# One of the weight sums of the seven-product pieces of the down projections and the last gate is made during the MLP halves, kept in DRAM, and read back into the weight piece

## The chip, the cores and the metric

One core of one Trainium2 chip runs the program. The metric is the device time of one execution in microseconds, lower is better. Of several executions the median is given.

## The reference

One encoder layer on 256 tokens of 2048 features, all in fp32. The parts that matter here:

```python
merged = jax.nn.sigmoid(ga) * (ya @ w_branch_a[i]) + jax.nn.sigmoid(gb) * (yb @ w_branch_b[i])
x = x + merged @ w_out[i]
hf = rms_norm(x, ffn_norm[i])
g = dwconv_centred(hf @ w_ffn_gate[i], conv_w[i], conv_b[i])
x = x + (jax.nn.gelu(g) * (hf @ w_ffn_up[i])) @ w_ffn_down[i]
gate_p = jax.nn.sigmoid(rms_norm(x, ple_norm[i]) @ w_ple_gate[i])
x = x + gate_p * (p[i] @ w_ple_proj[i])
```

Ahead of these stand the combined input projection and two kinds of windowed attention (ya, yb); a last rms norm follows. The feed-forward width is 5632.

## The kernel before, in words

**The stream of weights.** All weights lie in DRAM as 258 pieces of 128 x 2048 fp32 (1 MB, sixteen blocks of 128 x 128), in the order in which they are used. SyncE's DMA queue (SP) loads them into three buffers `raw` (L245); `produce` asks for piece p + 2 when it starts on piece p. A piece is cut into units, and each unit is split into two halves that TensorE can multiply in one pass: ScalarE (ACT) makes the high half (L265), VectorE (DVE) the low half, the rest (L266). The split units lie in two rings: "u" (tiles uh, ul) has 6 units, "v" (vh, vl) has 2. When TensorE has used a unit, `drop` frees its place and `pump` splits the next one. So ScalarE and VectorE run ahead of TensorE by what the rings hold, and no further.

**Stages in order.** A (projection and attention); B0 to B3 (the gates of the two branches), each followed by ba and bb (the branch projections); D0, D1 (the output projection and the residual); E0 (first half of the MLP's gate and up products) and F00, F01 (its down projection); E1, F10, F11 the same for the second half; pp0, pp1 (the projection of p); G0, G2, G3 (the last gate). In E a product uses one piece, 16 blocks, with a 512-wide and a 256-wide matmul for each; `mlp` then gathers it and, after every second one, does the convolution, gelu and the product of gate and up on VectorE and ScalarE.

**Pieces of seven products.** In B, D, F, G0 a piece holds two by two quarters of 128 x 512. `quad_stage` uses either eight products of quarters, kind "s", or seven, kind "S": the Winograd form of Strassen's method, where three of the seven use sums of weight quarters and four use sums of the moving side (tile S, made by `sums_of`). The sums of weights are made in place in `raw` by three subtractions on VectorE, once the plain quarters have been split (L258 to L260): first T1 and T3 (1024 wide), then T2 and the negative of T4 (512 wide each). The units that hold sums go through the ring "v". Each product is three matmuls (`thirds`, L366 to L368), so a seven-product piece is 21 matmuls of 512 columns. Of the 11 pieces of each F stage five are "S" (`DOWN`), of the 8 of G0 four (`ALT`).

**What sets the order.** The program text gives an order of emission; work can be put off to a place in a later stage with `at((stage, i, k), f)`. A scheduler then puts each engine's instructions in a fixed row by what each depends on and its own estimates, and may take one far ahead of its place in the text where its inputs and its buffer are free. On the chip each engine runs its row in order. Tiles with the same tag share a buffer and wait for each other. `act2` holds two rows of the MLP's activations, `S4` the moving sums of a pair of pieces.

Of the kernel before, what the change touches and what calls it, by code (L numbers as in the profile page):

```python
# [94 lines left out]
ALT = "SsSsSsSs"  # L95
DOWN = "SsSsSsSsSss"
FIRST_GATES = "ssssSsSs"
# [13 lines left out]
def _pieces():  # L111
# [29 lines left out]
    for half in range(2):  # L141
        names = {"g": "w_ffn_gate", "u": "w_ffn_up"}
        jobs = [(names[kind], f) for kind, f in _ffn(half)]
        joint = 0 if half else JOINT
        e = [(name, k, f) for k in range(KC) for name, f in jobs[:joint]]
        e += [(name, k, f) for name, f in jobs[joint:] for k in range(KC)]
        blocks("E%d" % half, e)
        for s in range(2):
            quads("F%d%d" % (half, s), ("w_ffn_down", 2 * s * WIDE), ("w_ffn_down", (2 * s + 1) * WIDE),
                  DOWN, half * FHALF)  # L150
# [14 lines left out]
def _unit_list():  # L165

    units, of = [], []
    for p, (kind, _) in enumerate(_PIECES):
        if p == 0:
            cuts = [("n", a * P, b * P) for a, b in ((0, 1), (1, 4), (4, 7), (7, 11), (11, PIECE))]  # L170
        elif kind == "S":
            cuts = [("n", 0, WIDE), ("n", 2 * WIDE, 4 * WIDE), ("T13", 0, 2 * WIDE), ("T24", 2 * WIDE, 4 * WIDE)]
        else:
            cuts = [("n", 0, 2 * WIDE), ("n", 2 * WIDE, 4 * WIDE)]
        of.append(list(range(len(units), len(units) + len(cuts))))
        units += [(p, *cut) for cut in cuts]
    return units, of
# [11 lines left out]
def _encoder(ctx: ExitStack, tc, xt, pt, xrow, cols, gainrow, table, onehot, mask, ident_in, wts, out):  # L189
# [13 lines left out]
    def bank(which, *shape):  # L203
# [7 lines left out]
        return ps.tile(list(shape) or [P, 2 * T], F32, name="bank", tag="b%d" % which, bufs=1)  # L211

    flat = big.tile([P, KC + KC * T], F32, name="x", tag="R1")
    x = flat[:, KC:].rearrange("p (k t) -> p k t", t=T)
# [27 lines left out]
    def load(r, a=0, b=PIECE):  # L242
        if a == 0:
            raws[r] = wpool.tile([P, PIECE * P], F32, name="raw", bufs=3)
        nc.sync.dma_start(raws[r][:, a * P:b * P], wts[r][:, a * P:b * P])  # L245
        state["raw"] = r + 1

    def produce():
# [7 lines left out]
        if kind == "T13":  # L256
            q = [raw[:, i * WIDE:(i + 1) * WIDE] for i in range(4)]
            nc.vector.tensor_tensor(raw[:, :2 * WIDE], raw[:, WIDE:3 * WIDE], raw[:, :2 * WIDE], op=ALU.subtract)  # L258
            nc.vector.tensor_tensor(q[2], q[2], q[0], op=ALU.subtract)
            nc.vector.tensor_tensor(q[3], q[3], q[2], op=ALU.subtract)  # L260
        src = raw[:, a:b]
# [3 lines left out]
        nc.scalar.activation(hi, src, AF.Copy)  # L265
        nc.vector.tensor_tensor(lo, src, hi.bitcast(F32), op=ALU.subtract)  # L266
        made[u] = (hi, lo)
        state["unit"] = u + 1
# [104 lines left out]
    def quad_stage(stage, moving, combos=None, tags=("M2", "M3", "M4", "P22")):  # L373
# [24 lines left out]
        for i, p in enumerate(pieces):  # L398
# [11 lines left out]
            else:  # L410
                s = combos(i)
                sums = [(s[:, 0, e], s[:, 1, e]) for e in range(4)]
                for g, (name, stationary, u, c, gone) in enumerate((
                        ("M1", part(a, 0), 0, 0, 0), ("M7", sums[2], 2, 1, None), ("M5", sums[0], 2, 0, 2),
                        ("M6", sums[1], 3, 0, None), ("M4", part(b, 1), 3, 1, 3),
                        ("M2", part(b, 0), 1, 1, None), ("M3", sums[3], 1, 0, 1))):
# [182 lines left out]
    def bias(h0, n):  # L599
# [8 lines left out]
    def view(a, offset, *dims):  # L608
        return bass.AP(tensor=a.tensor, offset=a.offset + offset, ap=[a.ap[0], *([step, n] for step, n in dims)])

# [357 lines left out]
    def mlp(kind, n, acc):  # L968
# [21 lines left out]
        else:  # L990
# [17 lines left out]
            pair = m // 2  # L1008
            if DOWN[pair] == "S":
                combos["act", pair] = sums_of(u, pair // 2)  # L1010
# [7 lines left out]
    def split_last():  # L1018
        for k in range(2):
# [3 lines left out]
            nc.vector.tensor_tensor(pl_[k], held["pr"][:, k], ph_[k].bitcast(F32), op=ALU.subtract)  # L1023

    for half in range(2):
        held["act"] = [big.tile([P, 16, 2 * T], FR, name="act", tag="R1"),
# [10 lines left out]
        turns["e"] = 0  # L1037
        for kind, n in jobs[joint:]:
            mlp(kind, n, product(stage, lambda k: hf[:, k, :], KC, "e"))
        if half:  # L1040
            at(("F10", 2, 0), load_last)
# [146 lines left out]
```

## Time and profile before

| | |
|---|---|
| median of 3 runs | 1457.01 us (1456.82 to 1458.02) |
| the profiled execution: its time | 1457.09 us |
| its span in the profile | 1455.3 us |
| mean granted clock of TensorE | 0.998 |
| HBM read, written | 279.49 MB, 2.14 MB |

The span is that from the first to the last instruction of the program; what lies around it is 1.8 us. In the profile a tile stands under its name in the program without its number, L266 is line 266 of the kernel shown. PE is TensorE's matmul, PEld its weight loads, SPq and ACTq the DMA issues of those queues. A group's row gives the count, then busy us and the mean ns of one, then the idle time of the engine in front of them with what ended it. A timeline row gives start, duration, engine, line, operation and tiles, and in brackets the idle time in front.

### The profile page before, as it was taken

How to read it: one execution, taken by the hardware profiler on the slowest of the kernel's cores; microseconds unless marked ns; L12 is line 12 of the kernel's file. 1: busy time of each engine (PE TensorE's matmuls, PEld its weight loads, DVE VectorE, ACT ScalarE, POOL GpSimd, SP SyncE). 2: the span in 40 equal slices, each digit the busy share in tenths (PEclk: the TensorE clock that was granted, in tenths of full speed). 3: DMA queues.
4: the chain of work that ended last, by engine and by line, in shares of the span. 5: the costliest groups of instructions: out<-in, count | busy, mean ns of one | idle time of the engine just before them, and what ended most of it. 6: DMA issues, size and time to landing. Idle time of an engine off the chain costs nothing.

```text
span 1455.3 us, 19303 instructions
## 1 busy us (share of the span) xinstructions
PE 1444.2 (99%) x7476; PEld 1234.3 (85%) x7476; DVE 1196.8 (82%) x1626; ACT 838.7 (58%) x1132; POOL 4.8 (0%) x9
## 2 busy tenths in 40 slices
PE   9999999999999999999999999999999999999997
PEld 8888888888888888888888888888888888888785
DVE  7677664679998989988787789987877778999994
ACT  7455544456555656666565565455655656565763
POOL 0000000000000000000000000000000000000000
PEclk9999999999999999999999999999999999999999
DMA  9653445535546456465555545465555554546462
GB/s 336 250 205 145 160 162 178 170 141 203 197 186 236 184 209 231 174 233 201 177 194 184 198 147 225 175 253 187 198 178 199 176 201 173 190 193 235 170 234 85
DMA packets 46455, 282.87 MB, mean 194 GB/s; under 512 B 4948, under 2 KB 9940, under 8 KB 14108
## 3 DMA queue, kind: packets, MB, share of 16 engines
q1 hardware_dynamic: 45644, 280.46, 52.8%
q8 instruction: 58, 0.95, 0.3%
q10 hardware_dynamic: 720, 1.19, 0.2%
q14 instruction: 33, 0.27, 0.1%
HBM read 279.49 MB, written 2.14 MB: 194 GB/s over the span
## 4 chain that ended last, share of the span: by engine, by line
PE 97%; DVE 1%; ACT 1%; issue 0%; DMA 0%; POOL 0%; POOLq 0%; DVEq 0%; SPq 0%; ACTq 0%
PE bank L309 29%; PE bank L316 15%; PE bank L366 14%; PE bank L367 14%; PE bank L368 14%; PE bank L355 2%; PE bank L357 2%; PE bank L293 2%; PE bank L356 2%; PE bank L294 1%; PE bank L861 1%; PE bank L678 0%; PE bank L626 0%; PE bank L625 0%; PE bank L624 0%
## 5 line engine op out<-in xcount | busy, mean ns | idle before, releaser
L265 ACT ACTIVATE uh<-raw 128x1024 fp32r<-128x1024 f32 (+2 forms) x519 | 523.1, 1015 | 394.0 <-PE bank L309 163.8
L266 DVE TENSOR_TENSOR ul<-raw,uh 128x1024 fp32r<-128x1024 f32 (+2 forms) x519 | 594.9, 1166 | 162.6 <-issue 81.0
L309 PE MATMUL bank<-hf,uh 128*128 128x512 f32 x1408 | 336.3, 391 | 0.0
L309 PEld LDWEIGHTS bank<-hf,uh 128*128 128x128 f32 x1408 | 258.9, 188 | 50.1
L316 PEld LDWEIGHTS bank<-hf,ul 128*128 128x128 f32 x1408 | 180.4, 191 | 6.7
L316 PE MATMUL bank<-hf,ul 128*128 128x256 f32 x1408 | 182.8, 283 | 0.0
L265 ACT ACTIVATE vh<-raw 128x1024 fp32r<-128x1024 f32 x92 | 97.0, 1056 | 42.4 <-DVE raw L258 22.9
L266 DVE TENSOR_TENSOR vl<-raw,vh 128x1024 fp32r<-128x1024 f32 x92 | 111.8, 1218 | 0.3
L309 PE MATMUL bank<-hs,uh 128*128 128x512 f32 x432 | 103.6, 392 | 0.0
L447 ACT ACTIVATE t<-bank 128x256 f32<-128x256 f32 x122 | 46.5, 383 | 97.4 <-PE bank L316 86.5
L309 PEld LDWEIGHTS bank<-hs,uh 128*128 128x128 f32 x432 | 79.5, 188 | 15.6
L366 PE MATMUL bank<-uh,act 128*128 128x512 f32 x232 | 90.4, 390 | 0.0
L367 PE MATMUL bank<-ul,act 128*128 128x512 f32 x232 | 90.4, 390 | 0.0
L368 PE MATMUL bank<-uh,act 128*128 128x512 f32 x232 | 90.2, 390 | 0.0
L366 PE MATMUL bank<-uh,hs 128*128 128x512 f32 x172 | 67.3, 391 | 0.0
L368 PE MATMUL bank<-uh,hs 128*128 128x512 f32 x172 | 67.2, 391 | 0.0
L367 PE MATMUL bank<-ul,hs 128*128 128x512 f32 x172 | 67.0, 389 | 0.0
L316 PE MATMUL bank<-hs,ul 128*128 128x256 f32 x432 | 56.6, 284 | 0.0
L258 DVE TENSOR_TENSOR raw<-raw 128x1024 f32<-128x1024 f32 x46 | 56.1, 1220 | 0.5
L316 PEld LDWEIGHTS bank<-hs,ul 128*128 128x128 f32 x432 | 54.5, 191 | 1.0
L367 PE MATMUL bank<-vl,S 128*128 128x512 f32 x138 | 54.0, 392 | 0.1
L366 PE MATMUL bank<-vh,S 128*128 128x512 f32 x138 | 54.1, 398 | 0.0
(242 smaller groups left out, 2229.4 us busy)
## 6 DMA issues: line engine op xcount, KB each, us to landing
raw<-in_wts SPq DMA_DIRECT2D x251, 1024.0 KB, 4.8
raw<-in_wts SPq DMA_DIRECT2D x12, 512.0 KB, 6.7
xr<-in_xrow SPq DMA_DIRECT2D x4, 512.0 KB, 8.2
x<-in_xt SPq DMA_DIRECT2D x13, 128.0 KB, 5.6
hb<-hold SPq DMA_DIRECT2D x3, 514.0 KB, 7.0
hb<-hold SPq DMA_DIRECT2D x2, 768.0 KB, 6.5
last<-in_gainrow SPq DMA_DIRECT2D x1, 1024.0 KB, 8.3
out<-xr SPq DMA_DIRECT2D x4, 256.0 KB, 2.6
```

Of the source, the lines that this page charges most:

```text
L258: nc.vector.tensor_tensor(raw[:, :2 * WIDE], raw[:, WIDE:3 * WIDE], raw[:, :2 * WIDE], op=ALU.subtract)
L265: nc.scalar.activation(hi, src, AF.Copy)
L266: nc.vector.tensor_tensor(lo, src, hi.bitcast(F32), op=ALU.subtract)
L293: nc.tensor.matmul(acc, hi[:, w], m, start=first, stop=False, skip_group_check=True)
L309: nc.tensor.matmul(acc, weights(u)[0][:, o * P:(o + 1) * P], m, start=first, stop=False, skip_group_check=True)
L316: nc.tensor.matmul(acc[:, T:], weights(u)[1][:, o * P:(o + 1) * P], m[:, :T], start=False, stop=last, skip_group_check=True)
L355: nc.tensor.matmul(acc[:, :n * P], xh, hi, start=(k == 0), stop=False)
L356: nc.tensor.matmul(acc[:, :n * P], xh, lo, start=False, stop=False)
L366: nc.tensor.matmul(acc, sh, wh, start=first, stop=False)
L367: nc.tensor.matmul(acc, sh, wl, start=False, stop=False)
L368: nc.tensor.matmul(acc, sl, wh, start=False, stop=last)
L447: keep(nc.scalar.activation(t, acc[:, T:], AF.Copy, scale=scale))
```

## The change

The seven-product pieces of F00, F01, F10, F11 and G0 become kind "Z"; those of B and D stay "S". A "Z" piece lies in DRAM as W12, W11, W22, W21. While an MLP half runs, each "Z" piece that follows it (10 in the first half, 14 in the second) is treated in two column halves by `sum_ahead`: SP loads 128 x 3 x 256 of the first three quarters into a tile `ahead` (384 KB), VectorE makes W22 - W12 + W11 = T2 with two 256-wide operations, and ScalarE's queue stores the 128 x 256 result in a DRAM tile (128 KB). The tiles take the buffers `act2` and `S4` by turns. When the piece itself is loaded, SP brings its last three quarters and, in a second DMA, the stored T2 in the place of W12, which is not needed by itself. From T2 the other three sums follow with two operations: T3 = T2 - W11 (512 wide), and W22 - T2 and W21 - T2 together (1024 wide). The two units of sums then hold T2, T3 and T1, -T4, so the products M5 and M6 change places.

```diff
-DOWN = "SsSsSsSsSss"
+DOWN = ("ZsZsZsZsZss", "ZsZsZsZsZss")
+LASTS = 30
...
-            pieces.append((c, [(n0, a), (n1, a), (n1, b), (n0, b)]))
+            pieces.append((c, [(n1, a), (n0, a), (n1, b), (n0, b)] if c == "Z" else
+                           [(n0, a), (n1, a), (n1, b), (n0, b)]))
...
-    quads("G0", ("w_ple_gate", 0), ("w_ple_gate", WIDE), ALT)
+    quads("G0", ("w_ple_gate", 0), ("w_ple_gate", WIDE), ALT.replace("S", "Z"))
...
+        elif kind == "Z":
+            cuts = [("n", WIDE, 2 * WIDE), ("n", 2 * WIDE, 4 * WIDE), ("T21", 0, 2 * WIDE), ("T03", 2 * WIDE, 4 * WIDE)]
...
+        if _PIECES[r][0] == "Z":
+            nc.sync.dma_start(raws[r][:, WIDE:], wts[r][:, WIDE:])
+            nc.sync.dma_start(raws[r][:, :WIDE], ahead.pop(r))
+        else:
+            nc.sync.dma_start(raws[r][:, a * P:b * P], wts[r][:, a * P:b * P])
...
+    def sum_ahead(p, h, tag):
+
+        cols = slice(h * T, (h + 1) * T)
+        if h == 0:
+            ahead[p] = dram.tile([P, WIDE], F32, name="ahead%d" % p)
+        q = held["tok"].tile([P, 3, T], F32, name="ahead", tag=tag)
+        nc.sync.dma_start(q, wts[p][:, :3 * WIDE].rearrange("p (q c) -> p q c", c=WIDE)[:, :, cols])
+
+        def add():
+            nc.vector.tensor_tensor(q[:, 0], q[:, 2], q[:, 0], op=ALU.subtract)
+            nc.vector.tensor_tensor(q[:, 0], q[:, 0], q[:, 1], op=ALU.add)
+
+        def store():
+            nc.scalar.dma_start(ahead[p][:, cols], q[:, 0])
+
+        return add, store
+
+    def sums_of_weights(raw):
+
+        q = [raw[:, i * WIDE:(i + 1) * WIDE] for i in range(4)]
+        nc.vector.tensor_tensor(q[1], q[0], q[1], op=ALU.subtract)
+        nc.vector.tensor_tensor(raw[:, 2 * WIDE:], raw[:, 2 * WIDE:], view(q[0], 0, (0, 2), (1, WIDE)), op=ALU.subtract)
...
+        todo = [(p, h) for p in sevens(half) for h in range(2)]
+        for i, (kind, n) in enumerate(jobs[joint:]):
+            if len(stores) > 1:
+                stores.pop(0)()
+            for f in adds:
+                at((stage, 8), f)
+            del adds[:]
+
+            def ask():
+                if todo and i > 1 and (i % 2 == 0 or i < LASTS):
+                    add, store = sum_ahead(*todo.pop(0), ("act2", "S4")[i % 2])
+                    adds.append(add)
+                    stores.append(store)
+                else:
+                    stores.append(lambda: None)
+            at((stage, 9), ask)
             mlp(kind, n, product(stage, lambda k: hf[:, k, :], KC, "e"))
```

In the rows below the changed kernel has line numbers of its own: L305 is the low split (before L266), L281 and L282 the two sums of a "Z" piece, L294 to L296 the three of an "S" piece (before L258 to L260), L270 and L271 the two operations of `sum_ahead`, L498 the gather (before L451).

VectorE in a down projection, one seven-product piece and the eight-product piece behind it; raw is the piece, ul and vl the low halves. Before, and now:

```order
L266 TENSOR_TENSOR ul<-raw,uh 128x512
L258 TENSOR_TENSOR raw<-raw 128x1024
L266 TENSOR_TENSOR ul<-raw,uh 128x1024
L259 TENSOR_TENSOR raw<-raw 128x512
L266 TENSOR_TENSOR vl<-raw,vh 128x1024
L260 TENSOR_TENSOR raw<-raw 128x512
L266 TENSOR_TENSOR ul<-raw,uh 128x1024 x2
L266 TENSOR_TENSOR vl<-raw,vh 128x1024
```

```order
L305 TENSOR_TENSOR ul<-raw,uh 128x512
L281 TENSOR_TENSOR raw<-raw 128x512
L305 TENSOR_TENSOR ul<-raw,uh 128x1024
L282 TENSOR_TENSOR raw<-raw 128x1024
L305 TENSOR_TENSOR vl<-raw,vh 128x1024
L305 TENSOR_TENSOR ul<-raw,uh 128x1024
L305 TENSOR_TENSOR vl<-raw,vh 128x1024
L305 TENSOR_TENSOR ul<-raw,uh 128x1024
```

Three operations on raw have become two, and both stand ahead of the first vl.

VectorE in stage D1, at the piece whose buffer is raw_5386; two of the MLP's early sums have been put there by the scheduler (ahead_6065 and ahead_7026, the tiles of `sum_ahead`). Before, and now:

```order
L266 TENSOR_TENSOR ul_5465<-raw_5386,uh_5464 128x512
L258 TENSOR_TENSOR raw_5386<-raw_5386 128x1024
L266 TENSOR_TENSOR ul_5469<-raw_5386,uh_5468 128x1024
L266 TENSOR_TENSOR vl_5485<-raw_5386,vh_5484 128x1024
L259 TENSOR_TENSOR raw_5386<-raw_5386 128x512
L266 TENSOR_TENSOR ul_5501<-raw_5422,uh_5500 128x1024
L260 TENSOR_TENSOR raw_5386<-raw_5386 128x512
```

```order
L305 TENSOR_TENSOR ul_5465<-raw_5386,uh_5464 128x512
L305 TENSOR_TENSOR ul_5469<-raw_5386,uh_5468 128x1024
L294 TENSOR_TENSOR raw_5386<-raw_5386 128x1024
L271 TENSOR_TENSOR ahead_6065<-ahead_6065 128x256
L295 TENSOR_TENSOR raw_5386<-raw_5386 128x512
L270 TENSOR_TENSOR ahead_7026<-ahead_7026 128x256
L296 TENSOR_TENSOR raw_5386<-raw_5386 128x512
L305 TENSOR_TENSOR vl_5485<-raw_5386,vh_5484 128x1024
```

The split vl_5485 has moved behind all three subtractions and two early sums. Ten of the first half's 20 pairs of sums stand this early, in stages from bb0 to D1 and at the start of E0; the other ten stand at the end of D1 and in E0.

VectorE in E1, two products; before, and now:

```order
L266 TENSOR_TENSOR ul_9368<-raw_9246,uh_9367 128x1024
L451 TENSOR_TENSOR gw_9371<-bank_9328,t_9372 128x256
L266 TENSOR_TENSOR ul_9403<-raw_9303,uh_9402 128x1024
L266 TENSOR_TENSOR ul_9415<-raw_9303,uh_9414 128x1024
L451 TENSOR_TENSOR pair_9418<-bank_9375,t_9419 128x256
```

```order
L305 TENSOR_TENSOR ul_9524<-raw_9391,uh_9523 128x1024
L498 TENSOR_TENSOR gw_9527<-bank_9479,t_9528 128x256
L270 TENSOR_TENSOR ahead_9730<-ahead_9730 128x256
L271 TENSOR_TENSOR ahead_9730<-ahead_9730 128x256
L270 TENSOR_TENSOR ahead_9782<-ahead_9782 128x256
L271 TENSOR_TENSOR ahead_9782<-ahead_9782 128x256
L305 TENSOR_TENSOR ul_9564<-raw_9453,uh_9563 128x1024
L305 TENSOR_TENSOR ul_9576<-raw_9453,uh_9575 128x1024
L498 TENSOR_TENSOR pair_9579<-bank_9532,t_9580 128x256
L270 TENSOR_TENSOR ahead_9835<-ahead_9835 128x256
```

Two pairs of sums stand ahead of one split, and the next one behind the following gather. The stores stand on ScalarE's row (that of ahead_9730 between uh_9563 and uh_9575), the loads on SP's, each between two weight pieces; ahead_9835 takes the buffer of ahead_9730.

More of the change, by code (lines that the diff above doesn't have):

```diff
@@ L260, in produce @@
             nc.vector.tensor_tensor(q[3], q[3], q[2], op=ALU.subtract)
+        behind = _PIECES[p][0] == "Z" == _PIECES[p - 1][0]
+        if kind == "T21" and not behind:
+            sums_of_weights(raw)
         src = raw[:, a:b]
@@ L266, in produce @@
         nc.vector.tensor_tensor(lo, src, hi.bitcast(F32), op=ALU.subtract)
+        if behind and u == _UNITS_OF[p][1]:
+            sums_of_weights(raw)
         made[u] = (hi, lo)
@@ L412, in quad_stage @@
                 sums = [(s[:, 0, e], s[:, 1, e]) for e in range(4)]
[L413 to L416, printed above, removed]
+                m1, m2, m4 = part(a, 0), part(b, 0), part(b, 1)
+                if kind == "S":
+                    todo = (("M1", m1, 0, 0, 0), ("M7", sums[2], 2, 1, None), ("M5", sums[0], 2, 0, 2),
+                            ("M6", sums[1], 3, 0, None), ("M4", m4, 3, 1, 3),
+                            ("M2", m2, 1, 1, None), ("M3", sums[3], 1, 0, 1))
+                else:
+                    todo = (("M1", m1, 0, 0, 0), ("M7", sums[2], 2, 1, None), ("M6", sums[1], 2, 0, 2),
+                            ("M5", sums[0], 3, 0, None), ("M4", m4, 3, 1, 3),
+                            ("M2", m2, 1, 1, None), ("M3", sums[3], 1, 0, 1))
+                for g, (name, stationary, u, c, gone) in enumerate(todo):
                     run_due(stage, i, g)
@@ L1008, in mlp @@
             pair = m // 2
-            if DOWN[pair] == "S":
+            if DOWN[half][pair] == "Z":
                 combos["act", pair] = sums_of(u, pair // 2)
@@ L1023, in split_last, with sevens @@
             nc.vector.tensor_tensor(pl_[k], held["pr"][:, k], ph_[k].bitcast(F32), op=ALU.subtract)
+    adds, stores = [], []
+    def sevens(half):
+        stages = ["F%d%d" % (half, j) for j in range(2)] + ["G0"] * half
+        return [p for stage in stages for p in _STAGES[stage] if _PIECES[p][0] == "Z"]
     for half in range(2):
@@ L1037, in _encoder @@
         turns["e"] = 0
-        for kind, n in jobs[joint:]:
+        todo = [(p, h) for p in sevens(half) for h in range(2)]
[10 more added lines that the diff above has]
+                    stores.append(store)
+                else:
+                    stores.append(lambda: None)
+            at((stage, 9), ask)
             mlp(kind, n, product(stage, lambda k: hf[:, k, :], KC, "e"))
+        assert not todo and not adds
+        while stores:
+            stores.pop(0)()
         if half:
```

8 lines of the change are left out of this document (4 added, 4 removed).

## The prediction

> **What bounds the kernel now.** I read the busy row and the chain first: who holds the end?
>
> ```profile
> PE 1444.2 (99%) x7476; PEld 1234.3 (85%) x7476; DVE 1196.8 (82%) x1626; ACT 838.7 (58%) x1132; POOL 4.8 (0%) x9
> ...
> PE 97%; DVE 1%; ACT 1%; issue 0%; DMA 0%; POOL 0%; POOLq 0%; DVEq 0%; SPq 0%; ACTq 0%
> ```
>
> TensorE holds 97% of the chain. A busy PE can hide waits, so the next view is that of waits, restricted to the weight loads of TensorE (each row: who waited, for whom, us in total, times, longest). From 870 to 1440 us:
>
> ```profile
> PEld bank L366 <- ACT last L1081: 0.8, 3, 0.4
> PEld bank L861 <- DVE xr L927: 0.6, 2, 0.4
> PEld bank L367 <- DVE vl L266: 0.5, 1, 0.5
> PEld bank L366 <- issue: 0.4, 2, 0.2
> PEld bank L861 <- PE bank L367: 0.2, 1, 0.2
> ```
>
> The list covers both down projections, the second MLP half and the last gate: TensorE waits 2.5 us there in all (0.8 + 0.6 + 0.5 + 0.4 + 0.2). That is the ceiling of what a lighter VectorE can give back. The third view is the table by stretches (us, then busy time of PE, PEld, DVE, ACT, POOL; clock; DMA share), mixer gates and branches, down of half 0, down of half 1; below it the second MLP half in a table of its own.
>
> ```profile
> 300.00:540.00 240.00, 240.00 (x1094) 198.73 (x1094) 220.82 (x278) 138.57 (x159) 0.00 (x0) 1.00 0.50 189
> 930.00:992.00 62.00, 62.00 (x279) 51.52 (x278) 56.26 (x60) 33.28 (x35) 0.00 (x0) 1.00 0.59 222
> 1280.00:1340.00 60.00, 60.00 (x272) 49.26 (x271) 59.52 (x76) 35.86 (x45) 0.00 (x0) 1.00 0.50 185
> ```
>
> ```profile
> 993.00:1216.00 223.00, 223.00 (x1283) 197.09 (x1282) 167.72 (x244) 129.73 (x176) 0.00 (x0) 1.00 0.53 192
> ```
>
> VectorE is nearly full in the down projections (59.52 of 60) and in the mixers (220.82 of 240), and has a quarter free in the MLP half. Still TensorE is at 60.00 of 60 everywhere: VectorE is full but ahead.
>
> **The change part by part.** *Removed.* In 24 pieces (10 per half, 4 of the last gate) three subtractions become two. The groups by form, 1220 to 1400 us:
>
> ```profile
> L258 DVE TENSOR_TENSOR raw<-raw 128x1024 f32<-128x1024 f32 x14 | 17.0, 1218 | 0.0
> L259 DVE TENSOR_TENSOR raw<-raw 128x512 f32<-128x512 f32 x14 | 9.6, 685 | 0.1
> L260 DVE TENSOR_TENSOR raw<-raw 128x512 f32<-128x512 f32 x14 | 9.6, 684 | 0.1
> ```
>
> Before: 1.22 + 0.69 + 0.68 = 2.59 us a piece. Now one 512 and one 1024 wide: 1.90. So 0.68 us x 24 = 16.4 us of VectorE go, all beside TensorE's work. What they can be worth is only the waits of the list above that VectorE ends: 0.5 (vl) and, as the queue in front of it shortens, 0.6 (xr). The other 1.4 us (ACT, issue, PE) don't hang on these sums. Value: 0 to 1.1 us gained; I take 0.6, since the vl wait stands directly behind the shortened sums and the xr one does not. M5 and M6 change places: the same 21 products a piece, 0.
>
> *Added on VectorE.* 48 pairs of 256-wide sums. Nearest row, a 256-wide sum in the MLP half, with the row that shows VectorE's free time there:
>
> ```profile
> L266 DVE TENSOR_TENSOR ul<-raw,uh 128x1024 fp32r<-128x1024 f32 x81 | 97.1, 1221 | 42.8 <-issue 40.9 <-PE bank L316 1.9
> ...
> L981 DVE SCALAR_TENSOR_TENSOR gw<-gw,cl 128x255 f32<-128x255 f32 x20 | 9.6, 482 | 9.1 <-ACT gw L980 9.1
> L451 DVE TENSOR_TENSOR gw<-bank,t 128x256 f32<-128x256 f32 x21 | 8.8, 418 | 0.0
> ```
>
> 2 x 0.418 = 0.84 us a pair, 40 us in all. Where they stand is decided by the order in front: 28 pairs in the second half, 10 in and around the first half, and the other 10, whose buffer (act2) is free early, as far ahead as the mixers.
>
> *The second MLP half.* The chain gives the length of a product there:
>
> ```profile
> 993.06 3.65 PE bank L309 x16
> 998.62 3.65 PE bank L309 x16
> ```
>
> One product is 5.56 us; 223 us are 40 of them; VectorE works 167.72 / 40 = 4.19 us in each, with a pair 5.03. So 0.53 us stay free, where 1.37 were. It must also stand for loads. A buffer's turn is store, then load; the DMA page has these sizes (out by ACT's queue, a piece of weights by SP's, rows of 1 KB from DRAM):
>
> ```profile
> raw<-in_wts SPq DMA_DIRECT2D x251, 1024.0 KB, 4.8
> ...
> hb<-hold SPq DMA_DIRECT2D x3, 514.0 KB, 7.0
> ...
> out<-xr ACTq DMA_DIRECT2D x4, 256.0 KB, 2.9
> ```
>
> The new store is 128 KB (at most 2.9 us), the new load 384 KB; it queues behind a piece of weights, so I take 4.8 since it goes through the same queue right behind one; the ends are 2.9 (the out row, smaller and alone) and 7.0 (the hb row, as short lines as the new load has). A turn is 7.7 us; the two buffers each have two products, 11.1 us, for it. The order is uneven, though. The place shown in front, in the profile of before (VectorE, then ScalarE, then TensorE):
>
> ```profile
> 1050.78 0.42 DVE L451 TENSOR_TENSOR gw<-bank,t 128x256 f32<-128x256 f32 x1
> 1053.43 2.36 DVE L266 TENSOR_TENSOR ul<-raw,uh 128x1024 fp32r<-128x1024 f32 x2 [2.23 <-issue]
> 1055.70 0.42 DVE L451 TENSOR_TENSOR pair<-bank,t 128x256 f32<-128x256 f32 x1
> 1058.99 2.36 DVE L266 TENSOR_TENSOR ul<-raw,uh 128x1024 fp32r<-128x1024 f32 x2 [2.87 <-issue]
> ```
>
> ```profile
> 1050.60 1.06 ACT L265 ACTIVATE uh<-raw 128x1024 fp32r<-128x1024 f32 x1 [1.46 <-PE bank L309]
> ```
>
> ```profile
> 1068.92 2.08 PE L316 MATMUL bank<-hf,ul 128*128 128x256 f32 x16
> ```
>
> The pair of ahead_9730 goes behind the gather of 1050.78 and ends at 1052.0; its store follows the split of 1050.60 on ScalarE, also 1052.0; 1052.0 + 7.7 = 1059.7 for the next load of that buffer, ahead_9835, whose pair is due at 1056.1, behind the gather of 1055.70. VectorE then stands 3.6 us and has 2.87 - 0.84 = 2.0 of it free: it comes 1.6 us late to the split of 1058.99. Behind the standing pair wait that split and, on ScalarE behind the store, the next uh. Who waits for them? The split of 1053.43 ends its first half at 1054.65 and is first used at 1068.92: a lead of 14.3 us. Cost: 0, hidden by that lead; without it, 1.6 us a time. SP's queue has 28 more issues there and weights behind each; a piece is asked for two products ahead of its split, 11.1 us, against 4.8 to land: 0. DMA: a share of 0.53 for 1024 KB a product, with 384 + 128 KB more about 0.8: it fits. ScalarE's store issues, as in
>
> ```profile
> 1444.82 0.90 ACTq L1132 DMA_DIRECT2D out<-xr  x2
> ```
>
> 0.45 us each, 21.6 us over an engine busy 58%: 0.
>
> By the Trainium skill's page DMA: Bandwidth & Descriptors, section Anatomy of one DMA, a DMA costs about 2.0 us fixed plus its bytes at 436 GB/s (a fit for GpSimd's path): an estimate of 2.3 us for the store and 2.9 for the load, a turn of 5.2. The 2.9 us of the out row for 256 KB agrees with it (2.6). With it the stand above would be 1.1 us, inside VectorE's free time, and the sum the same.
>
> *The mixers and the second residual stage.* Here the lead is thin. VectorE and TensorE at the tightest of the early pairs (ahead_6467, whose first sum goes ahead of the vl split):
>
> ```profile
> 445.92 1.75 ACT L265 ACTIVATE uh<-raw 128x512 fp32r<-128x512 f32 x2 [2.46 <-PE bank L368]
> ```
>
> ```profile
> 454.33 1.22 DVE L266 TENSOR_TENSOR vl<-raw,vh 128x1024 fp32r<-128x1024 f32 x1
> ```
>
> ```profile
> 458.87 0.39 PE L367 MATMUL bank<-vl,S 128*128 128x512 f32 x1
> ```
>
> The store before it follows the splits that end at 447.67; with 7.7 us the load lands at 455.4, where the pair is due at 454.4: 1.0 us of standing, a sum of 0.42, and the split is used 3.3 us after its end. Cost 0. The eight pairs from 300 to 540 us cost 6.7 us, out of 19.2 us that VectorE has free in the row of the mixers.
>
> In the second residual stage (D1) there is no lead. The place at piece raw_5386 shown in front, VectorE and then TensorE:
>
> ```profile
> 612.08 1.23 DVE L258 TENSOR_TENSOR raw<-raw 128x1024 f32<-128x1024 f32 x1
> 613.23 1.22 DVE L266 TENSOR_TENSOR ul<-raw,uh 128x1024 fp32r<-128x1024 f32 x1
> 614.50 1.23 DVE L266 TENSOR_TENSOR vl<-raw,vh 128x1024 fp32r<-128x1024 f32 x1
> ```
>
> ```profile
> 617.52 0.39 PE L367 MATMUL bank<-vl,S 128*128 128x512 f32 x1
> ```
>
> The vl split ends at 615.73 and is used at 617.52. Now the ul split, all three subtractions of the piece and two early sums stand ahead of it: from 612.08, 1.15 (the spacing of the first two rows) + 1.15 + 0.42 + 0.69 + 0.42 + 0.68 + 1.23 end at 617.8, 0.3 us late, and later if the ul split, now first, has to wait for its uh. One more early sum, in piece 104, adds up to 0.42. Value: 0 to 1.3 us lost (all three sums, 3 x 0.42); I take 0.6, the middle.
>
> **The sum.** Made against the profiled execution's 1457.09 us (a span of 1455.3 and 1.8 around it; 0.08 over the median of 1457.01). Minus 0.6, plus 0.6: 1457.1 us, the forecast's own range 1456.0 (all 1.1 gained, nothing lost) to 1458.4 (nothing gained, 1.3 lost). 0.2% of 1457 is 2.9 us, about what a measurement of this kernel can tell from no change.
>
> **The rivals.** *The mixers' VectorE stands for early loads: slower.* Its queue is in order, and 8 pairs stand in 240 us where the lead is 3.3 us. If each load comes 3.4 us later than the pair is due, the difference between
>
> ```profile
> xr<-in_xrow SPq DMA_DIRECT2D x4, 512.0 KB, 8.2
> ```
>
> and the 4.8 of a piece, that is 8 x 3.4 + 6.7 - 19.2 = 14.7 us late, less 3.3 of lead, 11.4 on TensorE: 1468.5. It decides from (19.2 + 3.3 - 6.7) / 8 = 2.0 us a pair on. For it: no spare buffer, SP's queue in order. Against: the 1.0 us worked out at the tightest pair. Chance 0.14.
>
> *The turn through DRAM paces the MLP halves: slower.* In four products VectorE works 20.1 us, stands 4.0 once (7.7 less two splits, a gather and a pair, 3.7) and 0.9 for ScalarE (twice the 0.46 of the L981 row): 25.0 against 22.2. Seven times 2.8 is 19.6; less the 14.3 of lead, 5.3: 1462.4. It decides when a product loses over 0.53 + 14.3 / 28 = 1.04 us to standing. Chance 0.10.
>
> *The relief is worth all waits from 870 us on: faster.* All 2.5 us go and the early sums cost nothing: 1454.6. For it: 59.52 of 60. Against: only 1.1 of them name VectorE. Chance 0.06.
>
> By the Trainium skill's fit of 5.2 us a turn, the first rival's load would land at 452.9, ahead of its pair, and both slower rivals would be less likely; no run here shows such a load yet, so I leave their chances.
>
> **How the numbers follow.** The forecast has 0.70. The range takes in it and the second rival, 0.80 together: 1456.0 to 1462.4. Faster by over 0.2%: half of the third rival, 0.03. Slower: the first two, 0.24. Within: 0.70 + 0.03 = 0.73.
>
> **What would show it.** The waits of the weight loads should have no vl row from 870 us on, and one or two rows more from 560 to 645. In the second MLP half TensorE's products should stay 5.56 us apart and VectorE go from 168 to about 191 us of 223 (28 x 0.84 more). Down of half 1 should show VectorE near 56 of 60. The prediction is wrong if TensorE waits over 3 us in any one stage, for ul or vl behind an early sum, or if the matmuls' spacing itself changes, which nothing here does.

## The result and the profile after

Five executions of the changed kernel have a median of 1471.96 us (1468.95 to 1474.79); those of the kernel before 1457.01. The ratio is 1.0101, 95% interval 1.0087 to 1.0116: slower by 1%, outside the range of the prediction. The profiled execution is the fastest of the five, 1468.95 us with a span of 1467.2; 11.9 us have to be found.

First the busy row and the chain of the page.

```profile
PE 1447.8 (99%) x7476; PEld 1234.4 (84%) x7476; DVE 1212.1 (83%) x1698; ACT 829.3 (57%) x1132; POOL 5.0 (0%) x9
...
PE 89%; DMA 4%; DVE 4%; issue 1%; ACT 1%; SPq 0%; POOLq 0%; POOL 0%; DVEq 0%; ACTq 0%
```

VectorE works 15 us more (1212.1 for 1196.8), TensorE as much as before, but the chain has lost 8% from TensorE to transfers and VectorE. Which stage? The table by stretches, second residual stage, down of half 0, second MLP half, down of half 1:

```profile
540.00:640.00 100.00, 98.61 (x459) 80.25 (x459) 96.50 (x122) 60.72 (x76) 0.00 (x0) 1.00 0.64 235
870.00:992.00 122.00, 122.00 (x547) 101.14 (x547) 107.56 (x116) 66.35 (x74) 0.00 (x0) 1.00 0.59 216
993.00:1216.00 223.00, 216.32 (x1218) 186.63 (x1217) 176.96 (x283) 116.65 (x167) 0.00 (x0) 1.00 0.67 240
1280.00:1340.00 60.00, 60.00 (x271) 49.54 (x271) 56.68 (x71) 36.23 (x46) 0.00 (x0) 1.00 0.53 193
```

In the 223 us of the second MLP half TensorE makes 1218 matmuls where it made 1283: 65 at 223 / 1283 = 0.174 us are 11.3 us. Around the second residual stage it is idle for 1.4 us of 100. In both down projections it is full (122.00 of 122, 60.00 of 60). So nearly all is lost in one place. Who is waited for there? The waits from 990 to 1160 us, of TensorE and of ScalarE, then of VectorE:

```profile
PEld bank L357 <- DVE ul L305: 9.3, 10, 2.0
...
PE bank L357 <- DVE ul L305: 5.9, 10, 1.6
...
PEld bank L350 <- ACT uh L304: 2.4, 4, 0.7
...
ACT uh L304 <- DMA raw<-in_wts: 0.4, 1, 0.4
```

```profile
DVE ahead L270 <- DMA ahead<-in_wts: 39.4, 15, 5.8
```

TensorE's weight loads wait 9.3 us for VectorE's low halves and 2.4 us for ScalarE's high halves, 11.7 us together. ScalarE itself waits only 0.4 us for weights. VectorE has stood 39.4 us, 15 times, at the first operation of an early sum for its load. One such place, at the pair that the prediction worked out (ahead_9835): VectorE, ScalarE, then SyncE's queue.

```profile
1067.90 0.41 DVE L498 TENSOR_TENSOR pair<-bank,t 128x256 f32<-128x256 f32 x1
1074.16 0.43 DVE L270 TENSOR_TENSOR ahead<-ahead 128x256 f32<-128x256 f32 x1 [5.85 <-DMA ahead<-in_wts]
1074.62 0.43 DVE L271 TENSOR_TENSOR ahead<-ahead 128x256 f32<-128x256 f32 x1
1074.96 2.35 DVE L305 TENSOR_TENSOR ul<-raw,uh 128x1024 fp32r<-128x1024 f32 x2
```

```profile
1064.14 0.33 ACTq L274 DMA_DIRECT2D ahead<-ahead  x1
...
1075.08 0.33 ACTq L274 DMA_DIRECT2D ahead<-ahead  x1
1075.51 0.38 ACT L494 ACTIVATE t<-bank 128x256 f32<-128x256 f32 x1 [7.05 <-DVE ahead L271]
```

```profile
1063.06 0.33 SPq L256 DMA_DIRECT2D raw<-in_wts  x1
1071.12 0.38 SPq L267 DMA_DIRECT2D ahead<-in_wts  x1
1071.59 0.44 SPq L256 DMA_DIRECT2D raw<-in_wts  x1
1072.13 0.38 SPq L267 DMA_DIRECT2D ahead<-in_wts  x1
```

VectorE is done with a gather at 1068.3, stands 5.85 us, makes the two sums and only then, at 1074.96, the next two low halves. Why so late? The store of the buffer's last result goes out at 1064.14. The next load of the same buffer is issued at 1071.12, 6.98 us later, and VectorE can add at 1074.16. A turn takes 10.0 us. SP stands meanwhile, and a piece of weights and the other load stand behind it; ScalarE stands 7.05 us behind the next store, which must wait for the sums. The chain view names the same two transfers, the store and the second load (start, us, what):

```profile
1064.14 6.92 DMA ahead<-ahead
...
1072.13 7.53 DMA ahead<-in_wts
1079.68 0.43 DVE ahead L270
```

The page's list of transfers has the medians of all 48:

```profile
ahead<-in_wts SPq DMA_DIRECT2D x48, 384.0 KB, 3.3
...
ahead<-ahead ACTq DMA_DIRECT2D x48, 128.0 KB, 4.7
```

In this kernel the store of 128 KB takes longer than the load of 384 KB.

In the residual stage the loss has another path. ScalarE's splits, then SP's queue, and last the same piece of weights in SP's queue of the kernel before:

```profile
579.48 2.01 ACT L304 ACTIVATE uh<-raw 128x1024 fp32r<-128x1024 f32 x2 [3.43 <-DMA raw<-in_wts]
```

```profile
563.59 0.56 SPq L963 DMA_DIRECT2D xr<-in_xrow  x1
572.44 0.39 SPq L267 DMA_DIRECT2D ahead<-in_wts  x1
572.92 0.44 SPq L256 DMA_DIRECT2D raw<-in_wts  x1
```

```profile
571.13 0.34 SPq L245 DMA_DIRECT2D raw<-in_wts  x1
```

An early load waits in SP's queue for a store that went out at 564.13; the piece of weights behind it leaves at 572.92 instead of 571.13 and lands too late for ScalarE. VectorE's splits of that piece come late with it, and TensorE's stop ends at 584.82 us with a copy of VectorE (c, L859) that stands behind them. The first MLP half begins 1.2 us later than before (641.27 for 640.09 us).

What was gained stands in the waits of TensorE's weight loads from 1230 to 1450 us:

```profile
PEld bank L407 <- ACT last L1149: 0.2, 1, 0.2
PEld bank L905 <- DVE xr L971: 0.2, 1, 0.2
```

With 0.3 us from 870 to 992, 0.7 are left of 2.5.

### The profile page after: what moved, and what is told of

Read it like the earlier page. It is cut to its first block, busy times and chain, and to the rows that moved or that the text cites. A ratio compares the mean times of both kernels' runs of the same rounds, so it can differ in the third digit from the quotient of the medians.

```text
span 1467.2 us, 19684 instructions
## 1 busy us (share of the span) xinstructions
PE 1447.8 (99%) x7476; PEld 1234.4 (84%) x7476; DVE 1212.1 (83%) x1698; ACT 829.3 (57%) x1132; POOL 5.0 (0%) x9
## 4 chain that ended last, share of the span: by engine, by line
PE 89%; DMA 4%; DVE 4%; issue 1%; ACT 1%; SPq 0%; POOLq 0%; POOL 0%; DVEq 0%; ACTq 0%
PE bank L350 25%; PE bank L408 14%; PE bank L409 14%; PE bank L407 14%; PE bank L357 13%; DMA ahead<-ahead 2%; PE bank L396 2%; PE bank L398 2%; PE bank L397 2%; PE bank L334 2%; DVE ul L305 1%; DMA ahead<-in_wts 1%; DMA raw<-in_wts 1%; PE bank L335 1%; PE bank L905 1%
## 5 line engine op out<-in xcount | busy, mean ns | idle before, releaser
L305 DVE TENSOR_TENSOR ul<-raw,uh 128x1024 fp32r<-128x1024 f32 (+2 forms) x519 | 595.4, 1166 | 114.7 <-ACT uh L304 67.4
L304 ACT ACTIVATE vh<-raw 128x1024 fp32r<-128x1024 f32 x92 | 96.6, 1056 | 43.0 <-DVE raw L294 11.3
L305 DVE TENSOR_TENSOR vl<-raw,vh 128x1024 fp32r<-128x1024 f32 x92 | 111.1, 1217 | 0.3
L270 DVE TENSOR_TENSOR ahead<-ahead 128x256 f32<-128x256 f32 x48 | 20.2, 420 | 54.4 <-DMA ahead<-in_wts 54.3
```

## The experiments

**The theories.** *The turn:* store, then load of the same buffer, take about 10 us in an uneven order. VectorE stands at the early sums in its fixed order, uses up its lead over TensorE, and from then on TensorE pays. Rivals: *the work* (VectorE has 0.84 us a pair too much), *the weights* (early loads crowd SP's queue and the DMA engines, and weights come late), *the issues* (ScalarE stands at the stores' issues and its splits come late). Each run is compared with the kernel before on the same chip (medians 1457.07 to 1457.12 us).

**Three buffers** for the turn.

```diff
-add, store = sum_ahead(*todo.pop(0), ("act2", "S4")[i % 2])
+add, store = sum_ahead(*todo.pop(0), ("act2", "S4", "S3" if i < 28 else "act2")[i % 3])
```

> The changed kernel, but the early sums take three buffers by turns instead of two (S3 as well, up to the 28th product, behind which it is needed for something else). The turn theory: VectorE stands in order at the early sums of the second MLP half because the next load of a buffer waits for its store; with three buffers store and load have 16.7 us (three products) instead of 11.1, against 8.0 to 11.5 of need (4.7 to 8.2 for the store, 3.3 for the load), so the standing goes and with it the 11.6 us that TensorE's rhythm loses there: 1459 to 1461 us, the row of VectorE's waits for the loads between 990 and 1160 us under 10 us instead of 39.4. The rival that VectorE has simply too much to do (0.84 us a pair): 1469 to 1473, as the changed kernel. The rival that weights arrive late because early loads use SP's queue and the DMA engines: 1469 to 1473. The rival that ScalarE's store issues delay its splits: 1469 to 1473.

Measured: 1467.68 us (ratio 1.0080, 1.0064 to 1.0097). A miss: about a third of the loss came back, not all. The profile is of one of the two longest of its six executions (1472.49 us). SP's queue:

```profile
1015.71 0.48 SPq L256 DMA_DIRECT2D raw<-in_wts  x1
1024.18 0.90 SPq L267 DMA_DIRECT2D ahead<-in_wts  x2
1025.13 0.48 SPq L256 DMA_DIRECT2D raw<-in_wts  x1
1025.77 0.37 SPq L267 DMA_DIRECT2D ahead<-in_wts  x1
```

SP's order is fixed too. The first load of the three waits at the head of the queue for its store, 8.1 us (that store went out at 1016.10), and the loads behind it go out with it. VectorE's waits for loads from 990 to 1160 us fell only from 39.4 us to these:

```profile
DVE ahead L270 <- DMA ahead<-in_wts: 34.3, 13, 6.7
```

A third buffer does little while one queue, in order, waits for the slowest of them. The scheduler also used it to put the 28 pairs of the second half closer together (from 971 to 1121 us, where the changed kernel has them from 982 to 1156), which works against the gain.

**The store out of the turn:** the result goes to a fourth quarter of the same buffer, so the next load waits for the sums alone.

```diff
-        q = held["tok"].tile([P, 3, T], F32, name="ahead", tag=tag)
-        nc.sync.dma_start(q, wts...)
+        if (tag, len(accs)) not in kept:
+            kept[tag, len(accs)] = held["tok"].tile([P, 4, T], F32, name="ahead", tag=tag)
+        q = kept[tag, len(accs)]
+        nc.sync.dma_start(q[:, :3], wts...)
...
-            nc.vector.tensor_tensor(q[:, 0], q[:, 0], q[:, 1], op=ALU.add)
+            nc.vector.tensor_tensor(q[:, 3], q[:, 0], q[:, 1], op=ALU.add)
...
-            nc.scalar.dma_start(ahead[p][:, cols], q[:, 0])
+            nc.scalar.dma_start(ahead[p][:, cols], q[:, 3])
```

> The changed kernel, but the second operation of an early sum writes the result to a fourth quarter of the same buffer (two buffers as before), so the next load waits only for the two operations and not for the store. The turn theory: the store leaves the turn, which becomes the 3.3 us of the load behind the sums: the loss in the second MLP half goes, 1459 to 1461 us. If instead the load alone is too late in SP's queue behind a piece of weights, the standing stays: 1467 to 1472. VectorE's work, or ScalarE's store issues, as the cause: nothing of them changes, 1469 to 1473.

Measured: 1459.32 us (1456.00 to 1461.54; 1.0014, 1.0005 to 1.0022). The same sums, loads, stores and queues, and 12.6 of the 14.9 us are back, although the scheduler put the pairs closer here as well (982 to 1116 us). The profile is of the shortest execution, 1456.00 us. The row of VectorE's waits from 990 to 1160 us, and SP's first row on early loads there:

```profile
DVE ahead L272 <- DMA ahead<-in_wts: 22.2, 11, 4.8
```

```profile
SPq L269 <- DMA ahead<-in_wts: 18.9, 8, 4.6
```

SP no longer waits for a store (before: `ahead<-ahead`, 99.9 us in 17 waits in the same stretch). VectorE still stands 22.2 us, and TensorE waits for a low half only once in that stage, 0.2 us.

**Sums without transfers,** and **no store,** both in the second half only.

```diff
...
-        nc.sync.dma_start(q, wts...)
+        if p < FIRST_OF_SECOND:
+            nc.sync.dma_start(q, wts...)
...
-            nc.scalar.dma_start(ahead[p][:, cols], q[:, 0])
+            if p < FIRST_OF_SECOND:
+                nc.scalar.dma_start(ahead[p][:, cols], q[:, 0])
```

The second run has the lower edit alone of these two. What is left out above them lets both read the pieces of the second half whole, and gives the first a buffer that is set once.

> The changed kernel, but in the second half the early sums are made on a buffer that is set once: no loads, no stores, and the pieces of the second half are read whole from the weights. It leaves out the true T2 of the second half (W12 stands in its place). VectorE's work is all there, the turn is gone. The turn theory: the loss in the second MLP half goes, what is left is the 1.9 us of the residual stages less the relief later: 1457 to 1460 us. VectorE's work as the cause: 1469 to 1473. The transfers as the cause (SP's queue, DMA engines): 1457 to 1460 as well.

> The changed kernel, but in the second half the early sums are loaded and made and never stored; the pieces of the second half are read whole from the weights. It leaves out the stored T2 of the second half (W12 stands in its place). The turn theory: without the store a turn is the load of 3.3 us alone and the loss goes, 1457 to 1461 us. The rival that the loads crowd SP's queue and the weights: the loads are all there, 1467 to 1472. The rival that ScalarE stands at its store issues in order: those are gone, 1457 to 1461 as well; it is told from the turn theory by the run that keeps the stores and takes them out of the turn. VectorE's work: 1469 to 1473.

Measured: 1458.74 us (1.0009, 1.0000 to 1.0017) and 1457.80 us (1.0005, 0.9997 to 1.0014). All of VectorE's added work costs nothing visible, so *the work* falls; the loads are there in the second run, so *the weights* fall for the MLP half, as the 0.4 us of ScalarE's wait for weights in the changed kernel had said. The issues are absent from both runs, but the run ahead of them keeps all 48, and there the loss in the MLP half is gone as well: *the issues* by themselves fall. (ScalarE's part of the loss, 2.4 us, goes with stands like the 7.05 us above, behind a store that must wait for late sums.) No store's row of VectorE's waits:

```profile
DVE ahead L271 <- DMA ahead<-in_wts: 15.3, 9, 4.1
```

**A store of a quarter of the size,** in the second half.

```diff
-            nc.scalar.dma_start(ahead[p][:, cols], q[:, 0])
+            n = T if p < FIRST_OF_SECOND else P // 2
+            nc.scalar.dma_start(ahead[p][:, h * T:h * T + n], q[:, 0, :n])
```

> The changed kernel, but in the second half only 64 of the 256 columns of an early sum are stored (32 KB for 128 KB, lines of 256 bytes), and the pieces of the second half are read whole from the weights; it leaves out the stored T2 of the second half (W12 stands in its place). The load still waits for the store. If the bytes make the store slow, it should land in 2 us or less and the loss in the second MLP half be small: 1458 to 1461 us. If a store that goes out beside 1 MB of weights takes its 5 to 8 us whatever its size, the loss stays: 1466 to 1472 us.

Measured: 1466.61 us (1459.09 to 1467.39; 1.0055, 1.0040 to 1.0070). Two thirds of the loss stay, and the page's list of transfers shows why:

```profile
ahead<-ahead ACTq DMA_DIRECT2D x20, 128.0 KB, 5.0
...
ahead<-ahead ACTq DMA_DIRECT2D x28, 32.0 KB, 4.2
```

The 20 whole stores are those of the first half, so the rows differ in place as well as in size. In the second half alone the trace gives 4.7 us in the middle for the whole store in the changed kernel and 4.2 for the quarter here: 0.5 us saved. VectorE stands almost as long:

```profile
DVE ahead L271 <- DMA ahead<-in_wts: 35.5, 13, 5.6
```

**Fewer pairs in the second MLP half:** the last gate as before, 20 pairs for 28.

```diff
-    quads("G0", ("w_ple_gate", 0), ("w_ple_gate", WIDE), ALT.replace("S", "Z"))
+    quads("G0", ("w_ple_gate", 0), ("w_ple_gate", WIDE), ALT)
```

> The changed kernel, but the last gate is as in the kernel before, so 20 early pairs stand in the second MLP half instead of 28. The turn theory, as an account: the first 11 or so eat the lead of 13 us, and each pair behind them costs TensorE what VectorE stands over its free time, about 11.6 / 17 = 0.7 us. With eight fewer of the paying ones 5 to 6 us of the 11.6 come back: 1464 to 1467 us. The rival that a loss of this size comes once, when the lead is gone, however many follow: 1469 to 1473 us.

Measured: 1465.14 us (1.0058, 1.0046 to 1.0070), 6.8 us back: the loss grows with the number of pairs. The single profile agrees less well: in the 223 us it lacks 52 matmuls, 9.0 us, so only 2.3 us of it are seen there, and the first long wait of a weight load (1.0 us) begins at 1052.7 us, where that of the changed kernel (0.7 us) begins at 1075.5. VectorE's waits for loads from 990 to 1160 us:

```profile
DVE ahead L270 <- DMA ahead<-in_wts: 31.9, 12, 5.6
```

The account by pairs holds in sign and roughly in size, not pair by pair.

**The pairs spread** over two of every three products.

```diff
-                if todo and i > 1 and (i % 2 == 0 or i < LASTS):
-                    add, store = sum_ahead(*todo.pop(0), ("act2", "S4")[i % 2])
+                if todo and i > 1 and (i % 3 != 1 if half else i % 2 == 0 or i < LASTS):
+                    add, store = sum_ahead(*todo.pop(0), ("act2", "S4")[len(todo) % 2])
```

> The changed kernel, but the 28 early pairs of the second MLP half stand in two of every three products up to the 43rd, instead of in each of 28 in a row: a buffer has 16.7 us for its turn instead of 11.1. The turn theory, as a rate: the standing of a pair stays but comes less often, VectorE regains 1.4 us in each product without one, and the lead of 13 us is not used up: 1458 to 1461 us. If the loads again go out in bunches behind one store, as with three buffers: 1464 to 1469 us.

Measured: 1473.53 us (1.0121, 1.0106 to 1.0135). A miss, and not a test of the rate: the scheduler takes work ahead of its place in the text, so the pairs stood as close as before, and VectorE's row of waits is nearly the old one:

```profile
DVE ahead L270 <- DMA ahead<-in_wts: 38.8, 14, 5.2
```

Only the last two pairs moved, to 1353 and 1364 us. Behind the last one TensorE waits once more, as its weight loads from 1340 to 1380 us show:

```profile
PEld bank L905 <- DVE xr L971: 3.2, 1, 3.2
```

**The early loads by GpSimd's queue.**

```diff
-        nc.sync.dma_start(q, wts...)
+        nc.gpsimd.dma_start(q, wts...)
```

> The changed kernel, but the loads of the early sums go out by GpSimd's queue instead of SyncE's, so that no piece of weights stands behind a load that waits for a store. The turn theory has two places: in the second residual stage the stop of 1.5 to 2.9 us comes from a piece of weights behind such a load and must go; in the second MLP half VectorE itself stands for the load, whatever its queue, and the loss stays: 1466 to 1471 us. The rival that late weights cause the loss in the MLP half as well: 1457 to 1460 us.

Measured: 1521.90 us (1.0441, 1.0422 to 1.0460), outside both. The rival of late weights is refuted again, since SP has no early load left and ScalarE waits for weights 2.5 us in all from 990 to 1160 us; but the loads took longer than in the changed kernel, and the pairs moved. The list of transfers, and VectorE's row of waits from 990 to 1160 us:

```profile
ahead<-in_wts POOLq DMA_DIRECT2D x48, 384.0 KB, 4.9
```

```profile
DVE ahead L270 <- DMA ahead<-in_wts: 45.4, 9, 7.6
```

5.0 us a time instead of 2.6. TensorE stands in the mixers and the residual stages too (one gap of 9.1 us at 596 us), so on the stop in the residual stage this run says nothing. What makes it 50 us longer than the changed kernel was not separated.

**The first half alone.**

```diff
-DOWN = ("ZsZsZsZsZss", "ZsZsZsZsZss")
+DOWN = ("ZsZsZsZsZss", "SsSsSsSsSss")
...
-    quads("G0", ..., ALT.replace("S", "Z"))
+    quads("G0", ..., ALT)
...
```

> The change in the first half only: the second half and the last gate are as in the kernel before. The turn theory: the 20 pairs of the first half are spread over the mixers, the residual stages and 40 products, VectorE's lead in the first MLP half never falls under 8 us, so nothing is lost there; what is left is the stop of 1.5 us in the second residual stage, where SP's queue stands 8.2 us for a store with a piece of weights behind the waiting load: 1458 to 1460 us. The rival that each early pair costs TensorE its share wherever it stands (15 us over 48 pairs): 20 x 0.31 = 6.2, 1463 us.

Measured: 1458.76 us (1.0013, 1.0005 to 1.0022). The 20 pairs of the first half cost 1.7 us together, not 6.2. The stop that was expected in the residual stage is not in its profile, though: the piece of weights goes out late there too (9.3 us behind the one before it, where the kernel before has 7.8), and TensorE waits only 0.5 us. From 300 to 660 us its weight loads wait 6.2 us in all, where they waited 3.6 before; the longest wait, 0.9 us, is in the mixers, at 426 us, and no run followed it up.

**The best version:** store out of the turn, and the first half's pairs kept out of the mixers and the residual stages (by the buffer S4 alone, which those stages use themselves).

```diff
-                    add, store = sum_ahead(*todo.pop(0), ("act2", "S4")[i % 2])
+                    add, store = sum_ahead(*todo.pop(0), ("act2", "S4")[i % 2 if half else 1], accs)
```

This stands on top of the edit with the fourth quarter.

> The result in a fourth quarter of the buffer, as in the run before, and the early sums of the first half through the buffer S4 alone, so that none is taken ahead into the mixers and the residual stages. The turn theory, with SP's queue as the cause in the second residual stage: no stop there, no loss in the second MLP half, and the relief of about 1 us in the last gate remains: 1455.5 to 1457 us. If the standing in the second MLP half is still too long in some executions: up to 1459.5, like the run with the fourth quarter.

Measured: 1456.42 us (1455.43 to 1458.38), ratio 0.9997, interval 0.9988 to 1.0006. It beats the changed kernel by 15.5 us; against the kernel before it is no difference that can be measured. VectorE's waits from 990 to 1160 us, and TensorE's weight loads from 870 to 1450 us:

```profile
DVE ahead L272 <- DMA ahead<-in_wts: 20.7, 12, 4.1
```

```profile
PEld bank L409 <- ACT last L1151: 0.4, 2, 0.2
PEld bank L409 <- issue: 0.3, 1, 0.3
PEld bank L907 <- DVE xr L973: 0.2, 1, 0.2
```

0.9 us of waits are left of 2.5: the relief that the change was able to give is there, and it is that small. That this version gains 2.9 us on the one with the fourth quarter alone agrees with the 1.7 us that the first half's pairs cost, but its edit moved all of them at once, so it does not say where they cost it.

## Why the prediction was wrong

**The step that failed** is in the second MLP half: "Cost: 0, hidden by that lead". The place was right (ahead_9835 was named), and so was the chain from store to load to standing pair; the lead of 14.3 us was counted as if it were there for each stand. It is one stock, and each stand that VectorE cannot make good draws on it. The timelines show it being used up, when the low splits of the second MLP half are paired in order with its matmuls on low halves. The lead is the time from the end of a split to its first use, in us, here for the first split of a product:

| TensorE at about, us | 1014 | 1025 | 1036 | 1059 | 1081 | lowest of all splits |
|---|---|---|---|---|---|---|
| kernel before | 14.3 | 14.3 | 14.2 | 14.2 | 14.2 | 12.8, several times |
| changed kernel | 14.3 | 9.8 | 5.4 | 3.4 | 0.1 | 0.05, first at 1076.2 |
| store out of the turn | 14.3 | 11.7 | 9.9 | 9.5 | 7.7 | 0.06, at 1131.0 |
| best version | 14.3 | 12.2 | 10.4 | 9.7 | 8.2 | 1.4, at 1131.3 |
| no store | 14.3 | 12.0 | 10.7 | 10.8 | 10.5 | 7.3, at 1133.0 |

In the changed kernel the lead stays under 2 us from 1076 to 1165 us, and there TensorE pays the 11.3 us. The second rival said just this, at a chance of 0.10 and with a price that was too small. Its terms, mis-sized:

- The store: "at most 2.9 us", from a row of 256 KB that leaves the kernel when no weights are loaded. Measured 4.7 in the middle; SP's longest wait for one was 8.2. The load: 4.8 taken, 3.3 measured in the middle, but 7.53 for the one that goes out behind a piece of weights.
- The turn: 7.7 us worked out, 10.0 measured at that place (1064.14 to 1074.16).
- Four products: 25.0 us worked out, 25.8 measured on average: the long stands end at 1048.3, 1074.2, 1100.5, 1126.3 and 1151.4 us. With 25.8 the rival's own sum is 7 x 3.6 - 14.3 = 10.9 us, against the 11.3 that are missing.

The point from which that rival decides, 1.04 us of standing per product, 29.1 us for 28, sorts the runs. Those under it (15.3 without store, 20.7 and 22.2 with the store out of the turn) lose nothing in the MLP half; those over it (34.3 with three buffers, 35.5 with the small store, 38.8 and 39.4) all lose 7 us or more (41 to 84 matmuls missing in the 223 us). The run with 20 pairs sorts itself too: 31.9 us of standing against 0.53 x 20 + 14.3 = 24.9, and a loss of 9.0. But any point from 22.2 to 31.9 us would sort them, and the lead shows that 29.1 is too high: with 22.2 us of standing, in pairs that stood closer, the lead came down to 0.06 us, so that run was at the edge and not 7 us away from it. The idea of the threshold held, its number was not tested; what the prediction lacked above all was a store's price beside weights.

By the Trainium skill's page DMA: Bandwidth & Descriptors, section Anatomy of one DMA, the estimates were 2.3 us for the store and 2.9 for the load. In the changed kernel the trace is near it for the load's median (3.3) and not for the store's (4.7). The same section says that most of a DMA's fixed time is the receipt of the last byte, heaviest when the target is HBM; that the small store still takes 4.2 us fits it in kind, but that is twice the fixed 2.0 us that it gives, and no run here measures the receipt.

**The other steps.**

- The pairs at 0.84 us: right (the two operations take 0.42 each), and hidden, as the run with sums alone shows.
- The three subtractions made two: taken 0.6 us gained, at most 1.1. Measured: the waits fell from 2.5 to 0.7 us, and to 0.9 in the best version. The rows of ACT and of issue, said not to hang on these sums, shrank too. In time it is no difference that can be measured, even in the best version.
- VectorE in the down projection of half 1: "near 56 of 60", 56.68 measured.
- "VectorE 168 to about 191 us of 223": 176.96, since it stood and fewer products fell into the 223 us; in the runs without loss it was 184.9 to 186.9, still under 191.
- The second residual stage, 0.3 us late at raw_5386, 0 to 1.3 in all: the vl split ended at 618.3 us (617.8 worked out), but nothing waited for it. TensorE, itself 1.3 us late by then, used it at 618.85 us. (Its wait of 0.4 us for a vl split is at 620.58, for the next one, where the kernel before waited 0.3.) What cost time in this stage was given at 0, SP's queue: there a piece of weights stood behind an early load, 1.4 us. That this is near the range of the other term is chance. Both runs with the store out of the turn issue that piece on time (571.17 and 571.20 us, 571.13 in the kernel before) and wait at most 0.4 us there. The runs that keep the queue as it was issue it late and TensorE's longest wait there lies between 0.5 and 2.9 us, so the late issue alone does not set the size of the stop.
- The mixers: no loss in the profile of after, and the first rival (1468.5 us) fell. That its number is near the measured one is chance: its loss would lie from 300 to 540 us.

**What stays open.** The median is 3.0 us above the profiled execution. The other four executions had a mean clock of 0.995 to 0.997 for its 0.998. The median one has 0.997, and 0.001 of 1469 are 1.5 us, half of the 3.0; the longest, 5.8 us above, has 0.995, and 0.003 are 4.4. The last section shows a way from a stop of TensorE to a lower clock, but those four left no trace, so this is argued and not shown, and the rest is open. And of a store's 4.7 us, how much is fixed and how much is other traffic was not separated by a run.

## What to carry to other kernels

A detour through DRAM has a turn, store and load of the same buffer, and its price must be taken from rows that run beside the same traffic; write the result where the next load does not need the place, and the store leaves the turn. An engine's lead is a stock: count what every stand takes from it over the whole stage, not whether it covers one. A waiting DMA issue holds up everything behind it in its queue, so a third buffer gave back only a third of the loss here, while one in-order queue waited for the slowest store.

## What the runs showed of the hardware

**A store's time went little with its size.** In the second half 128 KB took 4.7 us in the changed kernel and 32 KB 4.2 in the run with the small store. In the changed kernel, the trace gives issue and landing of 35 of the 48 stores: the eight that went out with no load in flight took 3.0 us in the middle, the eighteen with one load in flight 5.6, the nine with two 4.9.

**A stop of TensorE can halve its clock afterwards.** With three buffers its weight loads stopped for 3.0 us; the table by stretches ahead of, in and behind that:

```profile
1074.00:1077.00 3.00, 0.42 (x3) 0.03 (x1) 2.07 (x4) 0.76 (x1) 0.00 (x0) 0.94 1.03 417
1077.00:1080.00 3.00, 3.00 (x14) 3.00 (x15) 2.70 (x4) 2.47 (x4) 0.00 (x0) 0.50 0.68 182
1080.00:1106.00 26.00, 26.00 (x147) 22.86 (x147) 19.32 (x36) 12.65 (x18) 0.00 (x0) 1.00 0.72 251
```

The granted clock is 0.50 for the 3 us behind the stop: sixteen matmuls of 256 columns take 3.4 us there (from 1076.97 to 1080.36) instead of 1.9, so this stop of 3 us cost a further 1.5. A stop of 2.5 us in the run with sums alone was followed by the same: matmuls of 512 columns came every 0.43 us instead of 0.23, for 3.4 us. The trace of the spread pairs has stops of 2.9 and 3.2 us with the clock at 1.00 behind them, and that of the small store one of 2.4, so it doesn't always happen. The Trainium skill's page TensorE: Matmul & The Clock Gate, section What's actually happening, gives a free-running window of about 3.4 us, with the clock halved after one idle window. The half clock and its 3.4 us agree; stops of 2.5 and 3.0 us were enough, which is less than a whole window.

**The same load landed in 3.3 to 5.5 us, depending on the run.** 384 KB by SyncE's queue took 3.3 us in the middle in the changed kernel, 4.6 with no store in the second half and 5.5 with the store out of the turn; by GpSimd's queue it took 4.9. So no run here shows that GpSimd's queue is slower by itself.
